# Spread accumulating DMAs, later LayerNorm steps, products at the start and a new last tile in a hybrid decoder step

## The chip, the cores and the metric

The kernel runs on one core of a Trainium2 chip. The metric is device time in microseconds (us) of one execution. A core has a tensor engine (PE, TensorE), a vector engine (DVE), a scalar engine (ACT), a general engine (POOL, GpSimd) and a queue engine (SP), each with its own program, and 16 DMA engines that all of them share. DMAs issued by SP or ACT appear in the profile as hardware queues, those issued by POOL as a software queue.

## What is computed

One layer of a hybrid decoder is run on 2048 prompt tokens and on 64 sample tokens (8 sequences of 8), all in float32, with width 1024:

```python
proj = x @ w_in                                  # 1024 -> 3584: q, f, i, g, B, C, h
o    = hgrn2(silu(q), f, i, state)               # gated linear recurrence, 4 heads of 128
o    = o * rsqrt(mean(o*o) + 1e-6) * onorm_g * silu(g)
yc   = B * conv3(C * h)                          # causal, 3 taps
x    = layer_norm(ALPHA * x + concat(o, yc) @ w_out)
hid  = square(relu(x @ w_ff1))                   # 1024 -> 4096
x    = layer_norm(ALPHA * x + hid @ w_ff2)       # 4096 -> 1024
```

It returns x for both groups, the recurrence's new states and the last rows of the convolution's input.

## The kernel before

**Blocks and stages.** The prompt is taken in four blocks `b` of 512 tokens; block 1 takes the 64 sample tokens along. The mixers of a block are the stages m1 (q and f of the four heads), m2 (i and g) and m3 (the convolution), written as generators of 16, 16 and 24 steps. The loop over `main()` (L862) calls one step after another and, between them, advances the recurrence (`rec_step`), issues DMAs and runs one waiting step of the block before (`pump`). The output projection m4 follows, then the first LayerNorm, FF1 and FF2.

**float32 products.** Each operand is split into a high part (by ACT, L164 or L203) and a low part (by DVE, L165 or L210), and one product becomes three (L239 to L241, L245 to L247). A weight tile of 512 KB is loaded into a staging buffer `st` by SP (three buffers), split into `wh` and `wl` (four buffers each) and used once. `weights(i)` splits up to three tiles ahead of the one it returns, and SP's next load waits until DVE's split has freed a buffer. ACT and DVE run their programs strictly in order.

**Sums of weights.** FF1 and FF2 use products of sums of quarters of their weights (seven products in place of eight). The sums T1 to T4 of each of eight chunks lie in DRAM scratch, `T_a` for FF1 and `T_b` for FF2. They are made in block 0 by POOL's DMAs: a copy (L349), or a copy that accumulates (L347). For one chunk this is eight DMAs in a fixed order, `make_sums` (L342):

```python
(("T1","B11",False), ("T3","B22",False), ("T1","B12",True), ("T3","B12",True),
 ("T2","T3",False),  ("T2","B11",True),  ("T4","T2",False), ("T4","B21",True))
```

Four chunks are made together, step by step. `making` holds 64 of these DMAs (T_b of chunks 0 to 3 and T_a of chunks 4 to 7, in pairs) and `making1` 48 (T_b of chunks 4 to 7, then T_a of chunks 2 and 3). POOL can have eight such DMAs on their way; the next waits for the one eight before. `hold(x)` (L354) makes POOL read one element of `x` first, so that the DMAs behind it in POOL's queue start only when that value exists.

**When they are issued.** From step 6 of block 0's mixers two per step, until the 64 are used up. Then, behind each of the eight plain units of FF1's first part, two of `making1`; in FF2's first part one every third step (held by the split value `h`, three buffers); in FF1's second part one for each of the first eight units; the rest in block 1's mixers. T_b of chunks 0 to 3 is needed first in FF2's first part of block 0, T_a of chunks 4 to 7 in FF1's second part, T_b of chunks 4 to 7 in FF2's second part, and T_a of chunks 2 and 3 in block 1.

**Other work on POOL.** The powers -0.5 of the norms run on POOL: L720 for the recurrence's output (`out_stages`, four tokens' tiles a block, needed by m4), L271 for LayerNorms. They stand in the same queue as the DMAs.

**The second LayerNorm of a block** is not done at its end but pushed to `bg` as three steps a tile, `a1` (statistics, L266 to L271), `a2` (L287) and `a3` (L290 and the store), which `pump` runs in the next block's mixers on every second step, from step 0 on. A tile's buffer `tok` (eight in all) is free after the store, and m2 needs four or five of them.

**The end.** In block 3 the last chunk of FF2 is worked tile by tile: for each of four tiles and each half of the columns twelve products, an add to x (L1242) and half of the statistics (L266). `scaled` (ACT, L1364) and `stored` (L1370 on DVE, L1371 on POOL, store by SP) of a tile are called inside the next tile's turn. The last tile has its own lines, L1390 to L1398.

Of the kernel before, what the change touches and what calls it, by code (L numbers as in the profile page):

```python
# [14 lines left out]
ALU = mybir.AluOpType  # L15
# [46 lines left out]
def hybrid_step(ctx, tc, a, o):  # L62
# [294 lines left out]
    making1 = chain(make_sums(quarter2, range(NPART, NCH)), make_sums(quarter1, range(NPLAIN, NPART)))  # L357
# [42 lines left out]
    load_constants()  # L400
    carry = None


    for b in range(NB):
# [456 lines left out]

        for i, _ in enumerate(main()):  # L862
            rec_step()
            if b == 0 and i >= 6:
                if i == 6:

                    hold(ks[0][:, 0:1])
                next(making, 0)
                next(making, 0)
            if b == 1 and i % 2 == 0:  # L870
                next(making1, 0)
            if i >= 16 and i % (3 if samp else 4) == 0:
                rec_step()
            if i % 2 == 0:
                pump()
# [314 lines left out]

        for f, w in twice(pl["f0"], 0):
            ff1(f, w, [(0, 256)])
        drain()
# [4 lines left out]
        for f, w in twice(pl["f0"], 1):  # L1198
            ff1(f, w, [(256, ncols - 256)])
        drain()  # L1200
# [65 lines left out]
        for part, (ff1_units, ff2_units) in enumerate(pl["parts"]):  # L1266
            queue += [(step, c) for step, c, _ in ff2_units]
            for i, (step, c, u) in enumerate(ff1_units):
                if part == 1 and i in (4, 12):
                    norm_weights(1, (i // 8,))  # L1270
                if len(ff1_units) - 5 <= i < len(ff1_units) - 3:
                    prepare()
                if b == 0 and part == 0:
                    if i == 0:
                        for _ in making:
                            pass
                    ff1(step, weights(u), segs)
                    hold(values(c)[:, 0, 0, 0:1])
                    next(making1, 0)
                    next(making1, 0)  # L1280
                else:
                    ff1_product(step, c, weights(u))
                    if b == 0 and i < 8:
                        hold(values(c)[:, 0, 0, 0:1])
                        next(making1, 0)
# [18 lines left out]
            for n_, (step, c, u) in enumerate(ff2_units):  # L1304
# [21 lines left out]
                if b == 0 and part == 0 and n_ % 3 == 0:  # L1326
                    hold(h[:, 0, 0:1].bitcast(F32))
                    next(making1, 0)
# [23 lines left out]
        if b == NB - 1:  # L1352
# [13 lines left out]
            def stored(t):  # L1366
                for dh in range(2):
                    ds_ = slice(dh * 512, dh * 512 + 512)
                    z = x1[t][:, ds_]
                    v.tensor_tensor(z, z, lnb[:, 0, ds_], ALU.mult)  # L1370
                    g.tensor_tensor(z, z, lnb[:, 1, ds_], ALU.add)  # L1371
                    nc.sync.dma_start(dst(t)[:, ds_], z)

            for t in range(nt):
# [13 lines left out]
                ln_rstd(sts[t], P)  # L1388
            t, st = nt - 1, sts[nt - 1]
            v.scalar_tensor_tensor(st[:, 16:17], st[:, 12:13], -1.0, st[:, 15:16], ALU.mult, ALU.mult)  # L1390
            lo, hi = x1[t][:, :512], x1[t][:, 512:]
            s.activation(lo, lo, AF.Identity, scale=st[:, 15:16], bias=st[:, 16:17])
            v.scalar_tensor_tensor(hi, hi, st[:, 12:13], lnb[:, 0, 512:], ALU.subtract, ALU.mult)
            v.scalar_tensor_tensor(hi, hi, st[:, 15:16], lnb[:, 1, 512:], ALU.mult, ALU.add)
            nc.sync.dma_start(dst(t)[:, 512:], hi)
            v.tensor_tensor(lo, lo, lnb[:, 0, :512], ALU.mult)
            v.tensor_tensor(lo, lo, lnb[:, 1, :512], ALU.add)
            nc.scalar.dma_start(dst(t)[:, :512], lo)  # L1398
# [88 lines left out]
```

## Time and profile before

| | |
|---|---|
| median of 3 runs | 2387.24 us (2386.88 to 2389.86) |
| profiled execution | 2390.55 us |
| its span, first to last instruction | 2388.3 us |
| mean granted clock of TensorE | 0.994 |
| TensorE busy | 2340.0 us (98%) |
| DVE busy | 1785.6 us (75%) |
| ACT busy | 1233.5 us (52%) |
| POOL busy | 184.9 us (8%) |
| moved by DMA | 418.89 MB |

The times in the profile are those of the profiled execution, which took 3.3 us more than the median. A row of grouped instructions gives line, engine, operation, tiles (out<-in), busy time and the engine's idle time before them with what ended it. A wait is written "who <- for whom: us in total, times, longest". In a table by stage each engine has its busy time and its number of instructions, followed by the granted clock (1.00 is full speed), the DMA engines' mean busy share and the rate. A TensorE that runs at half clock counts as busy.

### The profile page before, as it was taken

The numbers are of one execution on the slowest core, as the hardware profiler recorded it, in microseconds if no ns is written. First come the engines' busy times: TensorE is split into PE (matmuls) and PEld (weight loads), VectorE is DVE, ScalarE is ACT, GpSimd is POOL, SyncE is SP. The second block draws the span as 40 slices with busy tenths as digits, with TensorE's granted clock in tenths as the row PEclk, the third lists the DMA queues.
The fourth block names the chain that finished last, engine by engine and source line by source line (L and its number), as shares of the span: only waits on it lengthen the run. The fifth ranks groups of instructions, "written<-read, shape, count | busy, mean of one in ns | idle before, by whom it ended". The sixth has DMA issues, their size and how long they took to land.

```text
span 2388.3 us, 38146 instructions
## 1 busy us (share of the span) xinstructions
PE 2340.0 (98%) x15036; PEld 2043.1 (86%) x15036; DVE 1785.6 (75%) x2832; ACT 1233.5 (52%) x1922; POOL 184.9 (8%) x234
## 2 busy tenths in 40 slices
PE   8999999999999999999999999999999999999998
PEld 7778978988879889879878788998988788998996
DVE  7856858578785677875688956888588975888678
ACT  5324645565423446646654234665665324665563
POOL 2230021100101110000000000000000001000001
PEclk9999999999999999999999999999999999999999
DMA  8997598867633644545553325456665325456663
GB/s 285 264 282 214 151 266 273 257 200 211 163 107 78 172 149 133 168 150 177 177 177 109 99 71 194 155 187 197 192 210 163 102 79 172 141 176 203 200 191 119
DMA packets 131507, 418.89 MB, mean 175 GB/s; under 512 B 13376, under 2 KB 17856, under 8 KB 131328
## 3 DMA queue, kind: packets, MB, share of 16 engines
q1 hardware_dynamic: 108880, 347.96, 45.7%
q0 software_dynamic: 22016, 67.71, 11.5%
q8 instruction: 118, 1.93, 0.3%
q10 hardware_dynamic: 432, 0.79, 0.1%
q14 instruction: 61, 0.50, 0.1%
HBM read 405.36 MB, written 69.77 MB: 199 GB/s over the span
## 4 chain that ended last, share of the span: by engine, by line
PE 50%; DVE 5%; DMA 1%; issue 1%; ACT 1%; POOL 0%; POOLq 0%; DVEq 0%; ACTq 0%
PE ps L247 9%; PE ps L245 9%; PE ps L246 9%; PE ps L239 6%; PE ps L240 6%; PE ps L241 6%; DVE wl L210 1%; DMA st<-in_w_ff 1%; PE ps L683 1%; PE ps L250 1%; PE ps L251 1%; DVE S L603 0%; DMA st<-T_b 0%; DVE l L165 0%; ACT wh L203 0%
## 5 line engine op out<-in xcount | busy, mean ns | idle before, releaser
L210 DVE TENSOR_TENSOR wl<-st,wh 128x1024 fp32r<-128x1024 f32 x580 | 707.4, 1221 | 173.3 <-ACT wh L203 171.2
L203 ACT ACTIVATE wh<-st 128x1024 fp32r<-128x1024 f32 x581 | 612.9, 1055 | 352.1 <-PE ps L247 125.6
L239 PE MATMUL ps<-X,wh 128*128 128x256 f32 (+2 forms) x1376 | 466.6, 339 | 9.8 <-ACT X L164 8.3
L240 PE MATMUL ps<-X,wh 128*128 128x256 f32 (+2 forms) x1376 | 456.8, 332 | 0.3 <-DVE X L165 0.3
L241 PE MATMUL ps<-X,wl 128*128 128x256 f32 (+2 forms) x1376 | 456.3, 332 | 0.0
L247 PE MATMUL ps<-wh,l 128*128 128x512 f32 x868 | 340.8, 393 | 9.0 <-DVE l L165 8.6
L245 PE MATMUL ps<-wh,h 128*128 128x512 f32 x868 | 338.2, 390 | 0.0
L246 PE MATMUL ps<-wl,h 128*128 128x512 f32 x868 | 338.0, 389 | 0.0
L239 PEld LDWEIGHTS ps<-X,wh 128*128 128x128 f32 x1376 | 263.0, 191 | 35.0 <-ACT X L164 9.3
L241 PEld LDWEIGHTS ps<-X,wl 128*128 128x128 f32 x1376 | 262.8, 191 | 22.0
L240 PEld LDWEIGHTS ps<-X,wh 128*128 128x128 f32 x1376 | 263.2, 191 | 21.3 <-DVE X L165 1.5
L247 PEld LDWEIGHTS ps<-wh,l 128*128 128x128 f32 x868 | 162.9, 188 | 52.4 <-DVE l L165 19.0
L246 PEld LDWEIGHTS ps<-wl,h 128*128 128x128 f32 x868 | 163.0, 188 | 34.0
L245 PEld LDWEIGHTS ps<-wh,h 128*128 128x128 f32 x868 | 163.0, 188 | 33.1 <-ACT h L164 0.4
L165 DVE TENSOR_TENSOR l<-raw,h 128x512 fp32r<-128x512 f32 x217 | 148.2, 683 | 9.8 <-ACT h L164 9.8
L247 PE MATMUL ps<-X,wl 128*128 128x256 f32 (+1 forms) x528 | 152.1, 288 | 0.2 <-DVE wl L210 0.2
L246 PE MATMUL ps<-X,wh 128*128 128x256 f32 (+1 forms) x528 | 151.9, 288 | 0.0
L245 PE MATMUL ps<-X,wh 128*128 128x256 f32 (+1 forms) x528 | 151.9, 288 | 0.0
L271 POOL TENSOR_TENSOR sm<-sm,nhalf 128x1 f32<-128x1 f32 (+1 forms) x34 | 34.7, 1020 | 1475.8 <-DVE sm L270 1429.6
L1147 DVE TENSOR_TENSOR raw<-raw,ps 128x512 f32<-128x512 f32 (+1 forms) x112 | 61.0, 571 | 104.9 <-PE ps L247 104.7
L164 ACT ACTIVATE h<-raw 128x512 fp32r<-128x512 f32 x217 | 133.7, 616 | 2.3 <-PE ps L246 2.2
L239 PE MATMUL ps<-wh,X 128*128 128x512 f32 x256 | 105.8, 413 | 2.8 <-DVE S L603 2.8
(259 smaller groups left out, 4369.2 us busy)
## 6 DMA issues: line engine op xcount, KB each, us to landing
st<-in_w_ff SPq DMA_DIRECT2D x227, 512.0 KB, 3.7
st<-T_b SPq DMA_DIRECT2D x124, 512.0 KB, 3.7
st<-in_w_in SPq DMA_DIRECT2D x110, 512.0 KB, 3.9
st<-T_a SPq DMA_DIRECT2D x88, 512.0 KB, 3.5
st<-in_w_out SPq DMA_DIRECT2D x56, 512.0 KB, 4.5
T_b<-in_w_ff POOLq DMA_DIRECT2D x48, 512.0 KB, 14.7
T_a<-in_w_ff POOLq DMA_DIRECT2D x36, 512.0 KB, 19.1
T_b<-T_b POOLq DMA_DIRECT2D x16, 512.0 KB, 12.9
```

The lines of the kernel that those rows point to most:

```text
L164: s.activation(hi, src, AF.Copy)
L165: later.append(lambda: v.tensor_tensor(lo, src, hi.bitcast(F32), ALU.subtract))
L203: s.activation(wh, st, AF.Copy)
L210: v.tensor_tensor(wl, st, wh.bitcast(F32), ALU.subtract)
L239: te.matmul(out, lh, rh, start=first, stop=False)
L240: te.matmul(out, lh, rl, start=False, stop=False)
L241: te.matmul(out, ll, rh, start=False, stop=last)
L245: te.matmul(out, lh, rh, start=first, stop=False, skip_group_check=True)
L246: te.matmul(out, lh, rl, start=False, stop=False, skip_group_check=True)
L247: te.matmul(out, ll, rh, start=False, stop=last, skip_group_check=True)
L271: g.tensor_tensor(st[:n, 15:16], st[:n, 14:15], nhalf[:n, 0:1], ALU.pow)
L1147: v.tensor_tensor(z, z, ps, (ALU.add, ALU.subtract)[op - 2])
```

## The change

It has four parts.

1. **DMAs of the sums.** Block 0's mixers issue only 26 steps' worth (52 DMAs). The other 12 of the first 64, and then T_b of chunks 4 to 7, are issued in FF1 (both passes of the plain first units, then FF1's first part) by `sums_beside`, one or two for a unit, each time held by a read of the value that the unit before wrote. In FF2's first part one is issued every third step. FF1's second part issues none; T_a of chunks 2 and 3 comes wholly in block 1's mixers (16 DMAs where 13 were).
2. **LayerNorm steps.** `pump` is called on every third step for as many tiles as must free their buffer before m2 (two tiles in block 1, one in block 2, none in block 3) and on every second step from step 26 on.
3. **Start.** TensorE gets twelve products of `ones` into a bank that nobody reads, ahead of the first weight.
4. **End.** `stored` adds on DVE instead of POOL, and the last tile is done by four passes of DVE, two that need only the mean and two that need the power, instead of L1390 to L1397.

The diff, cut to what matters:

```diff
-    making1 = chain(make_sums(quarter2, range(NPART, NCH)), make_sums(quarter1, range(NPLAIN, NPART)))
+    all_sums = chain(making, make_sums(quarter2, range(NPART, NCH)))
+    making1 = make_sums(quarter1, range(NPLAIN, NPART))
...
+    idle = PS((P, 4, P))
+    for _ in range(12):
+        te.matmul(idle, ones, ones.unsqueeze(1).to_broadcast([P, 4, P]), start=True, stop=True)
...
+        first_steps = 3 * max(0, len(bg) // 3 + nt + (1 if samp else 0) - 8)
...
-            if b == 0 and i >= 6:
+            if b == 0 and 6 <= i < 32:
...
-                next(making, 0)
-                next(making, 0)
+                next(all_sums, 0)
+                next(all_sums, 0)
...
-            if i % 2 == 0:
+            if i % 3 == 2 and first_steps:
+                first_steps -= 1
+                pump()
+            elif i >= 26 and i % 2 == 0:
                 pump()
...
+        def sums_beside(f, half, n):
+            if b == 0:
+                if made:
+                    hold(made.pop())
+                    for _ in range(n):
+                        next(all_sums, 0)
+                made.append(values(f // FC)[:, 2 * (f % FC // 2) + half, f % 2, 0:1])
...
             ff1(f, w, [(0, 256)])
+            sums_beside(f, 0, 1 + f % 2)
...
             ff1(f, w, [(256, ncols - 256)])
+            sums_beside(f, 1, 1 + f % 2)
...
-                    if i == 0:
-                        for _ in making:
-                            pass
                     ff1(step, weights(u), segs)
-                    hold(values(c)[:, 0, 0, 0:1])
-                    next(making1, 0)
-                    next(making1, 0)
+                    sums_beside(step, 1, 1 + i % 2)
                 else:
                     ff1_product(step, c, weights(u))
-                    if b == 0 and i < 8:
-                        hold(values(c)[:, 0, 0, 0:1])
-                        next(making1, 0)
...
-                if b == 0 and part == 0 and n_ % 3 == 0:
+                if b == 0 and part == 0 and n_ % 3 == 2:
                     hold(h[:, 0, 0:1].bitcast(F32))
-                    next(making1, 0)
+                    if next(all_sums, 0) == 0:
+                        next(making1, 0)
...
-                    g.tensor_tensor(z, z, lnb[:, 1, ds_], ALU.add)
+                    v.tensor_tensor(z, z, lnb[:, 1, ds_], ALU.add)
...
-            v.scalar_tensor_tensor(st[:, 16:17], st[:, 12:13], -1.0, st[:, 15:16], ALU.mult, ALU.mult)
-            lo, hi = x1[t][:, :512], x1[t][:, 512:]
-            s.activation(lo, lo, AF.Identity, scale=st[:, 15:16], bias=st[:, 16:17])
-            v.scalar_tensor_tensor(hi, hi, st[:, 12:13], lnb[:, 0, 512:], ALU.subtract, ALU.mult)
-            v.scalar_tensor_tensor(hi, hi, st[:, 15:16], lnb[:, 1, 512:], ALU.mult, ALU.add)
-            nc.sync.dma_start(dst(t)[:, 512:], hi)
-            v.tensor_tensor(lo, lo, lnb[:, 0, :512], ALU.mult)
-            v.tensor_tensor(lo, lo, lnb[:, 1, :512], ALU.add)
-            nc.scalar.dma_start(dst(t)[:, :512], lo)
+            halves = [slice(dh * 512, dh * 512 + 512) for dh in range(2)]
+            for ds_ in halves:
+                z = x1[t][:, ds_]
+                v.scalar_tensor_tensor(z, z, st[:, 12:13], lnb[:, 0, ds_], ALU.subtract, ALU.mult)
+            for ds_, queue_ in zip(halves, (nc.sync, nc.scalar)):
+                z = x1[t][:, ds_]
+                v.scalar_tensor_tensor(z, z, st[:, 15:16], lnb[:, 1, ds_], ALU.mult, ALU.add)
+                queue_.dma_start(dst(t)[:, ds_], z)
```

SP's order of loads and TensorE's order of products stay as they were, but for the twelve products. Three places show how the rest moves. The line numbers after the change are higher by 6 from the mixers on (L720 becomes L726, L634 becomes L640).

First, POOL's queue in block 0 where the powers of the recurrence's output stand (`sm`, `nhalf`). Before, they come behind the last of the 64 DMAs:

```order
L347 DMA T_b_121<-in_w_ff 128x1024
L347 DMA T_a_105<-in_w_ff 256x1x512
L347 DMA T_b_125<-in_w_ff 128x1024
L347 DMA T_a_109<-in_w_ff 256x1x512
L347 DMA T_b_129<-in_w_ff 128x1024
L347 DMA T_a_113<-in_w_ff 256x1x512
L720 TENSOR_TENSOR sm_1673<-sm_1673,nhalf 128x4
```

Now they come behind the 52nd:

```order
L349 DMA T_b_117<-T_b_115 128x1024
L349 DMA T_a_101<-T_a_99 128x1024
L349 DMA T_b_121<-T_b_119 128x1024
L349 DMA T_a_105<-T_a_103 128x1024
L726 TENSOR_TENSOR sm_1674<-sm_1674,nhalf 128x4
```

The powers moved ahead of 12 DMAs, four copies and eight that accumulate.

Second, POOL's queue at the turn from FF1's first part to FF2's first part in block 0 (`tick<-raw` is a read of an FF1 value, `tick<-h` one of a split value of FF2). Before:

```order
L354 TENSOR_TENSOR tick<-raw_3118 128x1
L347 DMA T_b_140<-in_w_ff 128x1024
L347 DMA T_b_144<-in_w_ff 128x1024
L354 TENSOR_TENSOR tick<-h_3063 128x1
L349 DMA T_b_131<-T_b_132 128x1024
L354 TENSOR_TENSOR tick<-h_3296 128x1
L349 DMA T_b_135<-T_b_136 128x1024
```

Now:

```order
L354 TENSOR_TENSOR tick<-raw_3155 128x1
L347 DMA T_b_135<-in_w_ff 128x1024
L347 DMA T_b_139<-in_w_ff 128x1024
L354 TENSOR_TENSOR tick<-h_3305 128x1
L347 DMA T_b_143<-in_w_ff 128x1024
L354 TENSOR_TENSOR tick<-h_3375 128x1
L349 DMA T_b_133<-T_b_131 128x1024
```

At the same point of FF2 the sums of chunks 4 to 7 are eight DMAs further on: 35 DMAs stand between the first LayerNorm's powers and the first read of h, where 16 stood.

Third, DVE in block 2's m1, where the recurrence of two heads is under way (`S` are its tiles, `wl` a weight's low part). Before, with a step of a LayerNorm in it:

```order
L455 TENSOR_TENSOR S_12700<-ps_12640,S_12701 128x512
L634 TENSOR_TENSOR S_12738<-S_12569,S_12620 128x512
L651 TENSOR_TENSOR S_12569<-S_12569,S_12619 128x512
L287 SCALAR_TENSOR_TENSOR tok_8321<-tok_8321,sm_12682,lnb 128x1024
L693 COPY_PREDICATED S_12464<-masks,ps_12762 32x4x2x8 x4
L613 TENSOR_TENSOR S_12386<-S_12386,S_12465 128x32x8
```

Now:

```order
L461 TENSOR_TENSOR S_12704<-ps_12650,S_12705 128x512
L640 TENSOR_TENSOR S_12742<-S_12581,S_12630 128x512
L657 TENSOR_TENSOR S_12581<-S_12581,S_12629 128x512
L699 COPY_PREDICATED S_12480<-masks,ps_12765 32x4x2x8 x4
L619 TENSOR_TENSOR S_12399<-S_12399,S_12481 128x32x8
```

The third tile's step has left this place; in block 2 only the first tile's three steps stay in m1.

More of the change, by code (lines that the diff above doesn't have):

```diff
@@ L400, in hybrid_step @@
     load_constants()
+    idle = PS((P, 4, P))
+    for _ in range(12):
+        te.matmul(idle, ones, ones.unsqueeze(1).to_broadcast([P, 4, P]), start=True, stop=True)
+    idle = None
     carry = None
@@ L1188, in hybrid_step @@
         to = dict(PRODUCTS)
+        made = []
+        def sums_beside(f, half, n):
[5 more added lines that the diff above has]
+                made.append(values(f // FC)[:, 2 * (f % FC // 2) + half, f % 2, 0:1])
         for f, w in twice(pl["f0"], 0):
             ff1(f, w, [(0, 256)])
+            sums_beside(f, 0, 1 + f % 2)
         drain()
```

## The prediction

> **What bounds the kernel now.** I read the page first, then TensorE's waits, then busy time by stage, and last the stages in which TensorE waited. The page's head:
>
> ```profile
> span 2388.3 us, 38146 instructions
> ...
> PE 2340.0 (98%) x15036; PEld 2043.1 (86%) x15036; DVE 1785.6 (75%) x2832; ACT 1233.5 (52%) x1922; POOL 184.9 (8%) x234
> ...
> q1 hardware_dynamic: 108880, 347.96, 45.7%
> q0 software_dynamic: 22016, 67.71, 11.5%
> ```
>
> TensorE is busy for all but 48.3 us of the span. Its own work stays (the change adds only 12 products at the start), so the gain can only come from those 48.3 us, and from stretches at half clock, which count as busy. TensorE's waits over the whole run (line waited for: us in total, times, longest) say where they are:
>
> ```profile
> ...
> PE ps L239 <- ACT X L164: 8.3, 2, 6.7
> PE ps L729 <- DVE S L725: 6.1, 2, 3.1
> PE ps L245 <- ACT raw L1145: 4.5, 2, 3.5
> PE ps L239 <- DVE S L603: 3.8, 3, 1.4
> PE ps L683 <- ACT tok L506: 2.7, 2, 1.4
> ```
>
> Busy time by stage places them. The columns are TensorE, weight loads, DVE, ACT, POOL, the granted clock, the DMA engines' share and GB/s.
>
> ```profile
> 172.30:180.00 7.70, 1.67 (x9) 0.93 (x7) 3.96 (x7) 5.52 (x26) 5.02 (x4) 0.82 1.08 193
> 177.20:184.00 6.80, 3.91 (x12) 3.23 (x13) 3.57 (x6) 6.13 (x24) 2.66 (x2) 0.50 1.06 219
> 256.00:297.00 41.00, 41.00 (x341) 40.78 (x340) 35.75 (x39) 29.29 (x50) 0.81 (x1) 1.00 0.50 147
> 345.00:360.00 15.00, 12.42 (x53) 9.41 (x52) 8.32 (x11) 6.32 (x8) 2.49 (x5) 1.00 1.04 319
> 440.00:460.00 20.00, 15.30 (x123) 14.63 (x122) 9.15 (x9) 12.78 (x16) 2.90 (x5) 1.00 0.95 303
> 1296.00:1338.00 42.00, 39.39 (x334) 30.41 (x332) 40.50 (x92) 12.60 (x20) 2.88 (x4) 1.00 0.28 88
> 1337.80:1344.60 6.80, 6.47 (x51) 5.27 (x52) 6.35 (x19) 2.69 (x5) 0.16 (x1) 0.50 0.43 157
> 1400.00:1450.00 50.00, 50.00 (x277) 43.02 (x276) 27.01 (x53) 22.05 (x66) 5.74 (x4) 1.00 0.36 114
> ```
>
> Three kinds of loss stand there. In block 0 the DMA engines are full (share 1.04 to 1.08) where TensorE waits. At 1296 DVE is full (40.50 of 42 us) with nearly idle DMA engines. And behind two of the waits the clock is 0.50 for 6.8 us.
>
> **1. The wait at 172.9 (-8.1 us).** POOL's timeline (start, duration, line, idle before):
>
> ```profile
> 145.30 0.52 POOL L349 DMA_DIRECT2D T_a<-T_a  x1 [4.09 <-DMA T_a<-in_w_ff]
> ...
> 172.32 1.05 POOL L347 DMA_DIRECT2D T_a<-in_w_ff  x1 [0.44 <-DMA T_a<-T_a]
> 172.91 2.52 POOL L720 TENSOR_TENSOR sm<-sm,nhalf 128x4 f32<-128x4 f32 x2
> ...
> ACT S L723 <- POOL sm L720: 12.9, 2, 10.8
> ```
>
> The power of L720 stands in POOL's queue behind all 64 sum DMAs; the last is issued at 172.32 and L720 runs right after. ACT had waited up to 10.8 us for it, and TensorE then 6.1 us in two waits. The change puts 52 DMAs ahead of it. The 52nd of before is issued at 145.30, so POOL is free 27 us earlier and the wait goes. What is late next is nothing of POOL's: in block 2 the same stage, without DMAs on POOL, has TensorE at 50.00 of 50 (row 1400). The half clock behind it costs at most 3.4 us; part of those 6.8 us is the second wait itself, so I take 2.0. 6.1 + 2.0 = 8.1; the least is 6.1.
>
> **2. The wait at 455 (-4.5 us).** At the start of FF1's second half three first-half sums (T_a) are still copied, and a weight tile that is due takes far longer to land than alone (DMA issues by stage: bytes, us to landing; the first row is 250 to 300, without software DMAs, the second 345 to 360, the third 445 to 460):
>
> ```profile
> st<-in_w_ff SPq DMA_DIRECT2D x14, 512.0 KB, 3.6
> ...
> st<-in_w_ff SPq DMA_DIRECT2D x4, 512.0 KB, 7.9
> ...
> st<-in_w_ff SPq DMA_DIRECT2D x3, 512.0 KB, 8.4
> ```
>
> 3.6 us become 8.4. After the change no sum is issued from the last step of FF2's first half until block 1, so this 4.5 us goes; at worst, if the last sums spill over, 2 of it.
>
> **3. The other end of that: FF1 and FF2 of block 0 (+4.0 us).** This is the cost, and the least certain term. The 12 delayed and 23 further sum DMAs now lie in FF1 of block 0, each held by a read of a value. The price of one: 11.5% of 2388 us is 275 us of all engines; less the outputs on that queue, 112 sums cost about 2.2 us each. A weight tile costs 45.7% of 2388 us over 347.96 MB, or 1.64 us for 512 KB. From 256 to 345 there are 89 us of DMA time, 93 at the measured 1.05. The weights take 20.5 (share 0.50 of 41 us) and then 8 times 1.64, 34 in all, and leave 59 us, or 27 sums. 35 are asked for. So about 8 sums, 18 us of DMA time, are still open when FF2 starts; before, only 16 sums had been asked for by then. FF1 itself has slack: its units wait for weights that were split three units earlier. FF2 has little, because the split h of a step stands on ACT behind the split of a weight three steps ahead, and that behind its landing:
>
> ```profile
> L210 DVE TENSOR_TENSOR wl<-st,wh 128x1024 fp32r<-128x1024 f32 x580 | 707.4, 1221 | 173.3 <-ACT wh L203 171.2
> ```
>
> One step is 12 products of 0.227 us, 2.72 us. A staging buffer is free again after 7.9 us of landing, ACT's pass, DVE's of 1.22 us and the next issue, about 10.5 us; with three of them one weight comes per 3.5 us, and 0.8 us is lost a step. Before, this cost 2.6 us in 345 to 360 (12.42 busy of 15). After, 18 us beside weights that take 1.64 of every 3.5 us last some 32 us, 9 steps, and about 7 us are lost. The difference is +4. It would be -2.6 if the backlog is gone by 345, and +15 if it stays through half of FF2. The Trainium skill (DMA: Bandwidth & Descriptors, Queues, rings and completion order) says each DMA engine goes round its queues packet by packet; by that rule alone a weight tile would get half an engine, an estimate of 5.2 us to landing, and the term would be about -2.6. The rows show 7.9, so they decide.
>
> **4. The LayerNorm steps moved out of m1 (-7.5 us).** In block 2's m1 stage DVE runs these beside the recurrence (1290 to 1340, busy us and mean ns):
>
> ```profile
> L290 DVE SCALAR_TENSOR_TENSOR tok<-tok,sm,lnb 128x1024 f32<-128x1024 f32 x3 | 3.8, 1262 | 0.0
> ...
> L266 DVE BATCH_NORM_STATS2 sm<-tok 128x6 f32<-128x512 f32 x4 | 2.6, 683 | 0.0
> L287 DVE SCALAR_TENSOR_TENSOR tok<-tok,sm,lnb 128x1024 f32<-128x1024 f32 x2 | 2.6, 1277 | 0.0
> ...
> ACT S L636 <- DVE S L634: 26.5, 6, 10.0
> ```
>
> 9 us of DVE's work there are LayerNorm, and ACT waits up to 10.0 us for DVE's L634, then TensorE for banks. After the change only one of the five tiles is normalised early in block 2, none in block 3; the rest starts at step 26. That frees about 8 us of DVE ahead of waits of 1.4 us each. The waits for L603 and L506 total 3.8 + 2.7; 1.0 of it is block 1's, so 5.5 us are at stake, and the half clock at 1337.8, at most 3.4, taken as 2.4 because the small products of this stage do not follow the clock alone: 7.9, of which I take 7.5. What hides the moved work: DVE has 23 us free in 1400 to 1450, and four tiles of 4.3 us (two statistics, L287, L290, small ones), 17 us, spread over steps 26 to 48. If that cover fails, a step of 1.26 us ahead of a bank's release costs up to 1.3 us, a few times. In block 1 six steps (two tiles) move to the end of m2, where one wait of 1.0 us stands already: 0, from -2 to +3.
>
> **5. The start (-2.2 us).** The first products:
>
> ```profile
> 6.69 0.80 PE L239 MATMUL ps<-X,wh 128*128 128x512 f32 x1 [6.69 <-ACT X L164]
> ...
> 8.73 4.30 DVE L165 TENSOR_TENSOR X<-tok,X 128x512 fp32r<-128x512 f32 x7 [1.29 <-ACT X L164]
> ...
> 11.78 0.63 PE L239 MATMUL ps<-X,wh 128*128 128x512 f32 x1
> ...
> 12.20 0.63 PE L240 MATMUL ps<-X,wh 128*128 128x512 f32 x1
> ...
> 13.91 0.39 PE L239 MATMUL ps<-X,wh 128*128 128x512 f32 x1
> ...
> 14.14 0.40 PE L240 MATMUL ps<-X,wh 128*128 128x512 f32 x1
> ```
>
> From 6.69 to 13.4 products stand 0.42 us apart, later 0.23. Twelve idle products at 0.42 take 5.1 us and fit into the 6.69 us of loading. Warm, the first 24 are bound by DVE, whose last split ends at 13.03: they end near 13.5 instead of 15.8. So -2.2; 0 if the clock falls back while the first tiles trickle in. The Trainium skill (TensorE: Matmul & The Clock Gate, Part 1) gives about 3.4 us of sustained activity until the full clock; by that, an estimate of 1.6 us is saved. The trace took 6.7 us, with gaps in the first half.
>
> **6. The tail (+1.7 us).** The end of the loop on DVE:
>
> ```profile
> 2373.79 0.68 DVE L1242 TENSOR_TENSOR tok<-tok,ps 128x512 f32<-128x512 f32 x1
> ...
> 2376.81 0.16 DVE L1363 SCALAR_TENSOR_TENSOR sm<-sm 128x1 f32<-128x1 f32 x1 [1.18 <-POOL sm L271]
> ...
> 2378.29 1.29 DVE L1370 TENSOR_TENSOR tok<-tok,lnb 128x512 f32<-128x512 f32 x2
> 2379.50 0.68 DVE L1242 TENSOR_TENSOR tok<-tok,ps 128x512 f32<-128x512 f32 x1
> ...
> 2384.72 0.69 DVE L1397 TENSOR_TENSOR tok<-tok,lnb 128x512 f32<-128x512 f32 x1
> ```
>
> A tile's turn is 5.71 us, a chain through POOL, ACT and DVE. Two more adds on DVE (1.3 us) stand in it; POOL answers some 0.5 us sooner without its own adds. Three turns add 1.3 + 0.9 + 0.9 = 3.1. The last tile took 5.9 us from its last sum at 2379.50 to the end of L1397. It now takes the two statistics, the small steps and four passes of 0.7, 4.6 us, of which the first two run while POOL makes the power: -1.4. Net +1.7, from -0.5 to +2.5.
>
> **The sum.** -8.1 - 4.5 + 4.0 - 7.5 + 0 - 2.2 + 1.7 = -16.6 us. The profiled execution took 2390.55 us (span 2388.3, 2.25 around it), 3.3 above the median 2387.24; 2390.55 - 16.6 = 2373.95, and from the median 2370.6.
>
> **Rivals.**
> A: *Only the queue is freed* (0.12). The m1 waits are the recurrence's own and stay, and the clock at the start falls back: -8.1 - 4.5 + 4.0 + 1.7 = -6.9, 2380. For it: the recurrence fills DVE at 1296 with 31 us besides LayerNorm. Against: the waits come only after three tiles' steps.
> B: *Slower* (0.05). POOL falls behind its DMAs in FF1, so its reads of h come late; h has three buffers, and ACT's next split waits for POOL, and the engines stay full through all of FF2. 28 steps at 0.8 us and a first wait of 10 to 15 us: 22 + 13, less the 2.6 of before, +32 in place of +4, 2399. It decides from about 12 sums open at FF2's start: eight may be on the way without holding POOL, and the balance of part 3 says eight. For it: that balance is close. Against: weights tolerate delay in FF1.
> C: *Nothing gained* (0.05). L720 waits for DVE's L719, not for its place in the queue, or DVE's moved steps cost in m2 what m1 gains: 2386. Against: L720 follows the last DMA within 0.6 us.
> The forecast has 0.78; within it term 3 alone moves the time by -6.6 to +11 us.
>
> **Range and chances.** About 0.2% (4.8 us) is what a measurement of this kernel can tell from no change. Low end: terms 3 and 4 at their best, 2370.6 - 6.6 - 2.4 - 2.2 is 2359. High end: term 3 at +15 (2381) or rival A (2380). Faster by over 0.2%, under 2382.5: the forecast but for 0.02 and A, 0.88; same 0.07 (C and the rest); slower 0.05 (B).
>
> **What would show it.** No TensorE wait for the out stage near 172 and no clock of 0.50 there; no wait for the first products of FF1's second half; more DMA share than 0.50 in 256 to 297, and the wait for l in 345 to 380 of about 7 us; DVE below full in block 2's m1 and no 0.50 there; products 0.23 us apart from 7 us on; a tile's turn of 6.6 us in the tail. I am wrong if the split of h waits for POOL's reads, or if TensorE waits appear in m2.

## The result and the profile after

The changed kernel took 2372.82 us (median of 4 runs, 2372.06 to 2376.58) against 2387.44 us before (4 runs, 2386.88 to 2389.86): 14.6 us less, ratio 0.993 with an interval of 0.9914 to 0.9946. The forecast was 2370.6 us. On a second occasion, with nine runs of the kernel before beside it, the changed kernel took 2372.81 us again, and the kernel before 2394.12 (2388.70 to 2398.96): ratio 0.9915 (0.9898 to 0.9932), 21.3 us less. The eight runs of the changed kernel on the two occasions lie within 4.9 us, the thirteen of the kernel before within 12.1, which turned out to be a part of the answer.

The profiled execution of the changed kernel took 2372.06 us (span 2370.3). The head of its page:

```profile
span 2370.3 us, 38176 instructions
...
PE 2335.7 (99%) x15048; PEld 2039.4 (86%) x15048; DVE 1789.1 (75%) x2837; ACT 1232.6 (52%) x1921; POOL 186.1 (8%) x234
```

TensorE's idle time fell from 48.3 to 34.6 us although it does 12 products more, and its busy time fell by 4.3 us all the same, because less of it runs at half clock (the mean granted clock rose from 0.994 to 0.997). Its waits over the whole run (line waited for: us in total, times, longest):

```profile
PE ps L247 <- DVE l L165: 10.3, 15, 1.5
PE ps L250 <- DVE hp L165: 3.2, 3, 1.3
PE ps L239 <- ACT X L164: 2.3, 2, 1.6
PE ps L689 <- DVE S L626: 1.9, 2, 1.0
...
PE ps L239 <- DVE S L609: 1.0, 1, 1.0
PE ps L705 <- DVE S L620: 1.0, 2, 0.5
```

The 6.1 us for the out stage, the 4.5 us for raw and the 2.7 us for tok are no longer there. The wait for l grew from 8.6 to 10.3. New are two lines that wait for the recurrence's S on DVE (L626 and L620), 2.9 us. (New line numbers from the mixers on are 6 higher than those of before.) The same stages as in the prediction, in the changed kernel:

```profile
164.00:175.00 11.00, 11.00 (x64) 9.40 (x63) 6.36 (x12) 7.35 (x28) 2.92 (x2) 1.00 0.16 49
245.00:286.00 41.00, 41.00 (x340) 40.74 (x339) 34.16 (x37) 27.80 (x47) 18.83 (x33) 1.00 1.03 286
334.00:372.00 38.00, 34.70 (x147) 26.72 (x146) 28.69 (x37) 19.48 (x25) 8.50 (x14) 1.00 0.94 301
432.00:447.00 15.00, 15.00 (x127) 15.00 (x127) 8.55 (x9) 10.94 (x15) 0.00 (x0) 1.00 0.69 241
1281.50:1323.50 42.00, 42.00 (x382) 33.01 (x381) 36.70 (x90) 15.38 (x23) 0.00 (x0) 1.00 0.28 89
1323.00:1330.00 7.00, 7.00 (x61) 5.53 (x60) 5.51 (x15) 1.06 (x1) 0.00 (x0) 1.00 0.00 1
1340.00:1372.00 32.00, 30.57 (x298) 23.17 (x296) 30.23 (x72) 9.34 (x13) 1.72 (x3) 1.00 0.31 99
```

TensorE (the first column behind the length) is full through the out stage, FF1, the start of FF1's second half and block 2's m1. FF1 of block 0 now carries the sums, with the DMA engines at 1.03 instead of 0.50. Two rows are not full: the start of FF2 (334 to 372) and, not foreseen in the sum, block 2's m2 (1340 to 1372), where DVE is busy for 30.23 of 32 us.

### A ledger by the same product

TensorE does the same products in the same order in all these kernels, but for the idle ones at the start. So the nth product from the end is the same work in every trace, and the difference of its start between two traces says what has been gained up to there. Below, each trace is set against that of the kernel before; a column is a stretch, by the times of the kernel before, and a number is what the stretch cost more (+) or less (-). "after" and "again" are two executions of the changed kernel; the first four rows do not have the spread sums, the others do.

```
stretch (us)   6-  160- 336- 430- 500- 690- 890- 920-  1320- 1372- 1590- 1740- 1880- 1930- 1960-  tail
               20  200  430  475  560  725  920  1320  1350  1400  1620  1800  1930  1960  2360
before          0    0    0    0    0    0    0    0     0     0     0     0     0     0     0     0
norm alone   -1.8 +1.8 +2.5 +4.2 +1.1    0    0    0   -6.0  +1.7  -0.9  +0.5  -3.1  +1.6  +0.4     0
start alone  -3.0 -0.8 +3.0 +2.4 +0.1 -1.5    0  +0.6  -2.8     0  -0.9  +1.0  +2.8     0     0     0
tail alone   -0.8 -0.9 +1.9 +2.1 -0.6 -1.5 -1.5  +0.3     0     0  -0.9  +1.6  +1.6     0     0  +2.0
sums alone   -1.0 -8.3 +4.3 -5.3 +0.7 -1.5    0  +0.2  -2.8     0  -0.9  +0.9  +1.5     0  +0.1     0
after        -3.0 -8.3 +3.4 -5.6 +0.3 -1.5    0  +0.1  -6.0  +1.7  -0.9  +0.5  -3.1  +1.6  +0.4  +2.4
again        -3.1 -8.3 +3.0 -5.6 +0.8 -1.5    0  +0.5  -6.0  +1.6  -0.9     0  -3.1  +1.6  +0.3  +2.5
```

The row "after" adds up to the difference of the spans, -18.0, but for rounding. Every step of the prediction has its column: start, out stage, FF2, FF1's second half, block 1 (690), block 2 (m1 from 1320, m2 from 1372), block 3 (m1 from 1880, m2 from 1930), tail. A row can also differ in a stretch that its edit does not touch, as -2.8 and +2.8 for "start alone" in blocks 2 and 3: that is how far one execution differs from another.

### The profile page after: what moved, and what is told of

Same layout as the page of the kernel before. It is cut to its first block, busy times and chain, and to the rows that moved or that the text cites. A ratio compares the mean times of both kernels' runs of the same rounds, so it can differ in the third digit from the quotient of the medians.

```text
span 2370.3 us, 38176 instructions
## 1 busy us (share of the span) xinstructions
PE 2335.7 (99%) x15048; PEld 2039.4 (86%) x15048; DVE 1789.1 (75%) x2837; ACT 1232.6 (52%) x1921; POOL 186.1 (8%) x234
## 4 chain that ended last, share of the span: by engine, by line
PE 53%; DVE 3%; issue 1%; DMA 1%; ACT 0%; POOL 0%; DVEq 0%; ACTq 0%; POOLq 0%
PE ps L247 10%; PE ps L245 9%; PE ps L246 9%; PE ps L239 7%; PE ps L240 7%; PE ps L241 7%; PE ps L689 1%; DVE wl L210 1%; PE ps L250 1%; PE ps L251 1%; DVE tok L1267 0%; DMA st<-T_b 0%; DVE l L165 0%; PE ps L783 0%; PE ps L780 0%
## 5 line engine op out<-in xcount | busy, mean ns | idle before, releaser
L247 PE MATMUL ps<-wh,l 128*128 128x512 f32 x868 | 341.5, 393 | 11.0 <-DVE l L165 10.3
```

Of the source, the lines that this page charges most:

```text
L247: te.matmul(out, ll, rh, start=False, stop=last, skip_group_check=True)
```

## The experiments

In each expectation P is the theory held first, Q and R are its rivals.

**The four parts, each alone on the kernel before.** They ran beside 29 runs of the kernel before (median 2393.91 us, 2385.59 to 2400.75). The four differences of the medians add up to 18.7 us (15.6 + 2.7 + 2.2 - 1.8), between the 14.6 and the 21.3 us of the whole change.

The spread of the sums alone (the mixers stop after 52 DMAs, the rest is held by reads in FF1 and FF2, as in the change's diff):

```
-            if b == 0 and i >= 6:
+            if b == 0 and 6 <= i < 32:
...
-                next(making, 0)
+                next(all_sums, 0)
...
+            sums_beside(f, 0, 1 + f % 2)
```

> The kernel before with the spread of the accumulating DMAs alone (old start, old LayerNorm steps, old tail). Theory P (the parts are independent, each brings what the two traces show in its stage when the same product is compared): the waits at 172.9 and 176.8 us and the half clock behind them go, -8.3; the FF2 stage of block 0 (340 to 420 us) loses 3.4 more than before; the waits at 448 and 455 us go, -5.5; nothing else moves. Sum -10.4 us, 2377 us. In block 2 the two waits near 1334 us and the 6.8 us of half clock behind them are still there. Rival Q (only the freed POOL queue counts, the other two terms depend on the moved start and cancel): -8.3 or less, 2379 to 2382 us. Rival R (delayed sums pile up in FF1): FF2's loss is 10 us or more, 2384 us.

Measured: 2378.32 us (2377.22 to 2378.88), ratio 0.9936 (0.9924 to 0.9948). By the trace it was as theory P said: -8.3, +4.3, -5.3, and both of block 2's waits still there (block 3's too), as the waits show:

```profile
PE ps L239 <- DVE S L604: 3.8, 3, 1.4
...
PE ps L684 <- ACT tok L507: 2.7, 2, 1.4
```

The half clock behind them did not come in this execution, though (-2.8). By the medians it gained 15.6 us, not 10.4, and its five runs lie within 1.7 us while the 29 of the kernel before lie over 15. Most of that kernel's unsteadiness sits in FF2 and FF1's second half of block 0: its four executions without the spread sums differ there by up to 6.6 us (336 to 475), while FF1's second half is within 0.3 us in every execution that spread the sums and put none of them there.

The times of the LayerNorm steps alone:

```
-            if i % 2 == 0:
+            if i % 3 == 2 and first_steps:
+                first_steps -= 1
+                pump()
+            elif i >= 26 and i % 2 == 0:
                 pump()
```

> The kernel before with the new times of the LayerNorm steps alone. Theory P: in m1 of block 2 -6.0 us and in its m2 +1.65 (new waits of 0.7 and 1.1 us on DVE's S where one step of 1.28 us stands ahead), in block 3 -3.1 and +1.6, together -5.8 us; block 1 is 0 as far as the steps go, and -1.5 if its wait near 706 us happens to lie across two clock windows. 2380 to 2381.6 us. Rival Q (the m1 waits are the recurrence's own and the traces differ by luck of the clock): at most -2 us, 2385 us.

Measured: 2391.18 us (2384.44 to 2394.43), ratio 0.9986 (0.9975 to 0.9997), so between 0.7 and 6 us. The time alone could hardly tell P from Q; the ledger does, with -6.0, +1.7, -3.1, +1.6 as P said and no -1.5 in block 1. The waits for ACT's tok (2.7 us) are gone, and of the 3.8 us for DVE's L603 only block 1's are left:

```profile
PE ps L239 <- DVE S L603: 1.0, 1, 1.0
```

Theory Q falls, though it is right in part: how much of the half clock follows these waits is luck. Block 2's m1 cost 2.8 us less than in the trace of before in two executions whose steps were not moved ("start alone", "sums alone"), and block 3's m1 1.5 to 2.8 us more in three of them. The wait of block 2 in the kernel before, and the same wait in "sums alone", where it lies across two windows and the clock stays:

```profile
1334.34:1337.75 3.41, 1.05 (x4) 0.49 (x3) 3.38 (x7) 0.57 (x2) 0.57 (x1) 1.00 0.53 154
```

```profile
1323.06:1326.47 3.41, 1.84 (x7) 0.86 (x6) 3.38 (x5) 0.00 (x0) 0.00 (x0) 1.00 0.28 103
1326.47:1329.88 3.41, 2.23 (x45) 1.93 (x46) 3.41 (x8) 3.19 (x6) 0.57 (x1) 1.00 0.52 209
```

Against the mean of the four executions whose steps were not moved, the moved steps bring 4.6 us in m1 of each of the two blocks, not 6.0 and 3.1. The waits of this kernel in the stretch that it does not touch were larger than in the trace of the kernel before (first that trace from 345 to 475 us, then this one):

```profile
PE ps L245 <- ACT raw L1145: 4.5, 2, 3.5
PE ps L247 <- DVE l L165: 2.6, 2, 1.4
```

```profile
PE ps L247 <- DVE l L165: 4.6, 4, 1.6
PE ps L245 <- ACT raw L1151: 3.7, 2, 2.9
PE ps L245 <- ACT wh L203: 1.7, 1, 1.7
```

The twelve idle products at the start alone:

```
+    idle = PS((P, 4, P))
+    for _ in range(12):
+        te.matmul(idle, ones, ones.unsqueeze(1).to_broadcast([P, 4, P]), start=True, stop=True)
+    idle = None
```

> The kernel before with the 12 idle products at the start alone. Theory P: the clock is full from about 5.4 us instead of 13.4, the 24th product starts near 12.2 us instead of 15.3: -3.0 us, 2384.4 us, and the distance stays the same to the end. Rival Q: a later wait takes it back (the wait at 172.9 us is for POOL's queue behind 64 DMAs, whose pace is not that of TensorE): the -3.0 at 20 us is gone at 185 us, 2387 us.

Measured: 2391.71 us (2385.68 to 2398.20), ratio 0.9993 (0.9982 to 1.0004), which decides nothing by itself. In the ledger the -3.0 are there at 20 us and still there behind the wait at 172 us (-3.8): P, not Q. But three other kernels without those products also stood 0.8 to 1.8 us ahead of the trace of before at 20 us: the clock rose at 10.3 to 12.6 us in them and at 13.4 in that one.

The new tail alone (the diff is the tail's part of the change):

```
-                    g.tensor_tensor(z, z, lnb[:, 1, ds_], ALU.add)
+                    v.tensor_tensor(z, z, lnb[:, 1, ds_], ALU.add)
```

> The kernel before with the new tail alone. Theory P: a tile's turn in the tail goes from 5.71 to 6.69 us, three turns and the first tile +3.4 us at the last tile's last sum, then -0.9 from there to the end: +2.5 us, 2389.9 us. Rival Q: the two adds that moved to DVE are hidden there and only the shorter last tile counts: -0.9 us, 2386.5 us.

Measured: 2395.69 us (2392.05 to 2398.79), ratio 1.0007 (0.9996 to 1.0018), which by itself tells nothing; from the start of the last product to the end it takes 11.66 us instead of 9.63, so +2.0. That is nearer to P's +2.5 than to Q's -0.9: this part makes the tail slower.

**Variants of the changed kernel.** They ran beside the unaltered one:

> The changed kernel unaltered, as the yardstick of the three variants that run beside it. Theory P (the waits of FF2 and FF1 in block 0 vary from execution to execution in the kernel before, and the spread of the sums ends that): its times lie within about 2 us of each other, near 2373 us, while those of the kernel before lie over some 10 us, and its gain is 17 to 20 us against this chip's before, not 14.6. Rival Q (the spread is the chip's and meets every kernel): the changed kernel's times lie over 10 us too.

Measured: 2372.81 us (three runs within 0.9 us, one at 2376.96) against 2394.12, so 21.3 us faster than the kernel before. P but for the one run: 4.7 us are more than its 2, and less than the 10.3 of the nine runs beside them.

The add of the tail back on POOL, the new last tile kept:

```
                     v.tensor_tensor(z, z, lnb[:, 0, ds_], ALU.mult)
-                    v.tensor_tensor(z, z, lnb[:, 1, ds_], ALU.add)
+                    g.tensor_tensor(z, z, lnb[:, 1, ds_], ALU.add)
```

> The changed kernel with the last add of a tail tile back on POOL, and the new last tile kept. Theory P (the adds moved to DVE stand in the chain of each tile's turn): the turn of a tile goes back to 5.7 us, the last sum follows the last product by 0.8 us instead of 4.2, and the last tile still takes 7.9 us from there: -3.4 us against the changed kernel. Rival Q (the turn is set by the reads of the tile's banks or the power on POOL): the adds on POOL delay POOL's power by 0.5 us a tile, and less than 1.5 us comes back.

Measured: 2367.77 us (2366.92 to 2368.29), ratio 0.9889 (0.9874 to 0.9905) to the kernel before. From the start of the last product to the end it takes 8.76 us, where the changed kernel takes 12.08: -3.3, as P said; the other 1.7 us lie in FF2. DVE's timeline of the changed kernel and of this variant (start, duration, line):

```profile
2355.71 0.68 DVE L1267 TENSOR_TENSOR tok<-tok,ps 128x512 f32<-128x512 f32 x1
...
2359.73 0.69 DVE L1388 TENSOR_TENSOR tok<-tok,lnb 128x512 f32<-128x512 f32 x1
...
2361.79 0.69 DVE L1389 TENSOR_TENSOR tok<-tok,lnb 128x512 f32<-128x512 f32 x1
2362.40 0.68 DVE L1267 TENSOR_TENSOR tok<-tok,ps 128x512 f32<-128x512 f32 x1
```

```profile
2351.49 0.68 DVE L1267 TENSOR_TENSOR tok<-tok,ps 128x512 f32<-128x512 f32 x1
...
2357.22 0.68 DVE L1267 TENSOR_TENSOR tok<-tok,ps 128x512 f32<-128x512 f32 x1
```

From the last sum of one tile to that of the next it is 6.69 us with the adds on DVE and 5.73 without. With the adds on DVE the last product starts 4.2 us before the last sum (0.8 us without): the sum stands behind four passes of the tile before (two of L1388, two of L1389).

The LayerNorm steps held until step 38, then one a step:

```
-            elif i >= 26 and i % 2 == 0:
+            elif i >= 38:
```

> The changed kernel with the LayerNorm steps that wait for step 26 held until step 38 (about 1371 us in block 2), then one a step instead of one in two. Theory P (the new waits near 1363 and 1367 us and near 1919 and 1923 us come of single LayerNorm steps that stand ahead of the recurrence while DVE is 95% busy): both pairs go, -1.65 and -1.58, -3.2 us against the changed kernel. Rival Q (the recurrence itself is late there by then, since m1 now runs at TensorE's pace): the waits stay or come back some 10 us later, 0 to -1 us; crowding after step 38 may even cost 1 to 3 us.

Measured: 2371.49 us (2369.44 to 2373.39). The pairs of waits in m2 are gone, and one new wait of the same size stands in each of the two blocks (block 2, 1340 to 1420 us; block 3 has the same row):

```profile
PE ps L735 <- DVE S L731: 1.5, 1, 1.5
```

So neither theory alone: the waits do come of the steps' place, and crowding them gave it all back.

The reads of h kept in FF2, their DMAs moved into FF1's second half:

```
                     hold(h[:, 0, 0:1].bitcast(F32))
-                    if next(all_sums, 0) == 0:
-                        next(making1, 0)
...
                     ff1_product(step, c, weights(u))
+                    if b == 0 and i >= 2:
+                        hold(values(c)[:, 0, 0, 0:1])
+                        next(all_sums, 0)
```

> The changed kernel with the reads of h by POOL kept in FF2 of block 0, but the sum DMAs that they release moved on into FF1's second half (ten of them, one a unit from the third on, each behind a read of a value). Theory P (FF2 loses time because its weight tiles land late beside sum DMAs): the backlog from FF1 still costs the waits up to 358 us, about 3.5 us, but the rest of FF2's loss (0.9 us at 405 and the 1.5 us around 362 to 372) goes; FF1's second half, which splits its weights three units ahead, takes the ten DMAs at no cost: -1.5 to -2.4 us. Rival Q (POOL's reads of h hold its buffers): FF2's loss of 5.6 us stays, 0. Rival R (sum DMAs in FF1's second half cost what they did in the kernel before, where three copies at its start made 3.7 us): +2 to +5 us.

Measured: 2381.09 us (2380.68 to 2383.38), 8.3 us slower than the changed kernel. FF2's column falls to -0.4 from +3.0 in the unaltered one, with POOL's reads still in place: the loss there is the DMAs, not the reads, as P said. In FF1's second half R was right, and worse: from -5.6 to +2.3 in 430 to 475 us, and +2.7 more in 500 to 560. Two of its weight tiles landed 15.1 us after their issue (median, 436 to 460 us) instead of 3.5 in the changed kernel (420 to 447 us), each kernel's row below, and TensorE waited for them:

```profile
st<-in_w_ff SPq DMA_DIRECT2D x2, 512.0 KB, 15.1
...
PE ps L245 <- ACT wh L203: 4.1, 1, 4.1
```

```profile
st<-in_w_ff SPq DMA_DIRECT2D x5, 512.0 KB, 3.5
```

Both tricks together, with the LayerNorm steps left out at 32 to 37 only:

```
-            elif i >= 26 and i % 2 == 0:
+            elif (26 <= i < 32 or i >= 38) and i % 2 == 0:
```

> The changed kernel with the last add of a tail tile on POOL as in the run with that alone, and with the LayerNorm steps of the mixers left out at steps 32 to 37 (they run at 26, 28, 30 and from 38 on, one in two as before). Theory P (one LayerNorm step, L287 of the second tile, stands ahead of the recurrence where DVE has no room, and in the run with all steps after 38 it was their crowding that made the new wait at L735): the pairs of waits near 1363 and 1919 us go and no wait of L735 appears: -3.2 us against the run with the add on POOL alone (2367.8), 2364.6 us. Rival Q (two of DVE's 8 to 12 us of moved steps must end up ahead of some bank's release wherever they stand): waits of the same 1.6 us a block show up elsewhere, 2367.5 us.

Measured: 2376.13 us (2372.15 to 2379.24), 8 us slower than the add on POOL alone. The pairs in m2 went, but behind the mixers 4.6 us were lost in block 2 and 6.9 in block 3, part of it at half clock. Neither theory had this. SP's queue shows it (1405 to 1432 us: start, duration, line; below it DVE's last LayerNorm step, and SP's wait for it):

```profile
1406.14 8.49 SPq L182 DMA_DIRECT2D st<-in_w_out  x2
1421.21 7.39 SPq L263 DMA_DIRECT2D lnb<-in_lnb  x2
...
1429.64 2.02 SPq L182 DMA_DIRECT2D st<-in_w_out  x3
```

```profile
1426.97 1.27 DVE L290 SCALAR_TENSOR_TENSOR tok<-tok,sm,lnb 64x1024 f32<-64x1024 f32 x1
```

```profile
SPq L263 <- DVE tok L290: 6.7, 1, 6.7
```

The second of the two reloads of lnb goes out as the last step that reads the old lnb (L290) ends, at 1428.2 us, and behind it in SP's queue stand weight tiles, three of them in this view, which TensorE then waits for. The LayerNorm steps have a deadline, and the change's own last step (L290 at 1413.45) meets it: its reloads are both out by 1418.4 us.

Steps at 26, 28, 30, 32, 38, 40, 42 to 46 and 48, so that none stands at 34 and 36 and the last is no later:

```
-            elif i >= 26 and i % 2 == 0:
+            elif i in (26, 28, 30, 32, 38, 40, 42, 43, 44, 45, 46, 48):
```

> The changed kernel with the last add of a tail tile on POOL, and LayerNorm steps at 26, 28, 30, 32, then at 38, 40, 42, 43, 44, 45, 46 and 48: none stands at 34 and 36, where the recurrence waited for DVE, and the last one is no later than in the changed kernel, so that the reload of lnb on SP's queue, which waits for the last reader, is no later either. Theory P (the moved steps cost where they stand ahead of the recurrence, and at the end where the reload of lnb and the weights behind it wait for them): the pairs near 1363 and 1919 us go, and neither the wait at L735 near 1407 nor the one near 1437 us appears: -3.2 us against the add on POOL alone (2367.8), 2364.6 us. Rival Q (DVE has no room for these steps anywhere between steps 32 and 48): a wait of 1 to 1.7 us a block comes back at another place, 2367 us or more.

Measured: 2366.91 us (2364.92 to 2371.11), ratio 0.9904 (0.9889 to 0.9918) to a kernel before of 2389.52 on that occasion. The m2 waits fell from 1.6 to 0.4 us in each of blocks 2 and 3, and no wait came back elsewhere in the mixers, -2.4 us by the trace: P, less a remainder. The time alone would have fitted Q (2367 or more); its FF2 happened to be 2.3 us slower than in the run with the add on POOL alone. This and that run are the best versions found; they can't be told apart.

64 sum DMAs in the mixers of block 0 again, in the changed kernel:

```
-            if b == 0 and 6 <= i < 32:
+            if b == 0 and 6 <= i < 38:
```

> The changed kernel with 64 sum DMAs in the mixers of block 0, as before, instead of 52 (the last 12 stand again ahead of the power of L726 in POOL's queue), and so 12 fewer in FF1 and FF2. Theory P (the wait at 172.9 us was the place in POOL's queue): the two waits and the half clock behind them return, +8.3 by 185 us; FF2's loss in 344 to 420 us, 3.4 to 5.6 us in the changed kernel, falls to 1 to 3 us, since fewer sums are open when it starts; sum +5 to +7, 2378 to 2380 us. Rival Q (the power waits for its input from DVE and the queue did not matter): nothing returns at 172.9 us, 2370 to 2373 us. Rival R (the loss of FF2 does not depend on how many sums FF1 has to carry): +8.3, 2381 us.

Measured: 2378.74 us (2373.27 to 2380.93), ratio 0.9942 (0.9927 to 0.9956): P. POOL's timeline of this variant, then that of the changed kernel:

```profile
166.62 0.81 POOL L347 DMA_DIRECT2D T_b<-in_w_ff  x1 [0.28 <-DMA T_b<-T_b]
167.82 1.05 POOL L347 DMA_DIRECT2D T_a<-in_w_ff  x1 [0.39 <-DMA T_a<-T_a]
168.41 2.54 POOL L726 TENSOR_TENSOR sm<-sm,nhalf 128x4 f32<-128x4 f32 x2
```

```profile
142.22 0.52 POOL L349 DMA_DIRECT2D T_a<-T_a  x1 [4.10 <-DMA T_a<-in_w_ff]
155.58 1.88 POOL L726 TENSOR_TENSOR sm<-sm,nhalf 128x4 f32<-128x4 f32 x1 [12.85 <-DVE sm L725]
```

In the first the power runs two at a time behind the last DMA, in the second POOL had been idle for 12.85 us when DVE's input came. The two waits (4.5 us) and the half clock came back, 7.0 us, and FF2's column fell to -0.9: with 12 sums fewer to carry, FF2 lost 3.9 us less than in the unaltered one, and its -0.9 lies below the 1.2 to 4.3 us of the eight executions that spread all of them.

Six idle products instead of twelve:

```
-    for _ in range(12):
+    for _ in range(6):
```

> The changed kernel with 6 idle products at the start instead of 12: they end near 3.6 us, and TensorE then rests until the first real product at 6.7. Theory P (the clock counts busy time in windows of 3.41 us, and a window with a rest in it does not raise it): the full clock comes only at 9 to 13 us, the 24th product starts at 14 to 15.3 us instead of 12.2, +2 to +3 us. Rival Q (some 2.5 us of products in the first window are enough to raise it and it stays up): 12.2 us, 0.

Measured: 2373.97 us in one run; at 20 us it stands 2.1 us behind the changed kernel. PE's timeline of it:

```profile
1.07 2.93 PE L405 MATMUL ps<-ones 128*128 128x512 f32 x6 [1.07 <-POOL ones L137]
...
11.75 0.63 PE L240 MATMUL ps<-X,wh 128*128 128x512 f32 x1
...
12.58 0.39 PE L239 MATMUL ps<-X,wh 128*128 128x512 f32 x1
```

The clock rose at 12.5 us, as late as with no idle products at all (10.3 to 13.4): P, by one run.

## Why the prediction was right, step by step

**1, the queue of POOL** (-8.1): -8.3, in every kernel with the spread sums, and undone by putting 12 DMAs back. Right in mechanism and size. Rival A (only this) falls with the LayerNorm run, rival C with the POOL timeline. C's 2386 us needed both of its conditions; with one of them its own terms give 2378 to 2379.

**2, the wait at 455** (-4.5): -5.6 against that trace. Its typical size is larger: in four executions without the spread sums the stretch cost 0, 4.2, 2.4 and 2.1 us against the trace, 2.2 on average, so the typical gain is 5.6 + 2.2, about 7.8 us. That it is the sum DMAs that delay the weights was shown by the run that put ten of them there.

**3, FF1 and FF2 of block 0** (+4.0): +3.4 against the trace. FF1 had the slack that was claimed (41.00 of 41). But the sizing failed in two ways. First, the eight open sums were not eight: at 334 us, where FF2 starts in the changed kernel, four were under way and two more of the 35 had yet to be issued, and in the kernel before, at 345, four were under way as well. So FF2 starts with six unfinished sums against four. POOL had waited for its own chain, one sum reading what another makes (second row: 30.0 us, one wait of 15.7 of them from 306 to 322 us; POOL's waits, 235 to 420 us):

```profile
POOL tick L354 <- ACT h L164: 48.7, 7, 10.3
POOL T_b L349 <- DMA T_b<-in_w_ff: 30.0, 7, 15.7
```

Ten more were issued in FF2 from 344 us on, eight of them behind reads of h, which waited for ACT (first row). Second, the trace of before was a lucky execution: without the spread sums FF2 cost 1.8 us more on average (0, 2.5, 3.0, 1.9), with them 2.7 (eight executions, 1.2 to 4.3). The typical price of the step is thus about 1 us, not 4; that this trace shows 3.4 is luck. The sign named for it, a wait for l of about 7 us, came out at 4.0 (335 to 420). Rival B, with ACT waiting for POOL's reads, did not happen: POOL waited for ACT. The Trainium skill's packet-by-packet rule (DMA: Bandwidth & Descriptors, Queues, rings and completion order) gave an estimate of 5.2 us to landing and -2.6 us; the tiles took 9.1 us at 334 to 349 us in the changed kernel:

```profile
st<-in_w_ff SPq DMA_DIRECT2D x4, 512.0 KB, 9.1
```

so the measurement decides against that estimate here; why the tiles take longer was not tried.

**4, the LayerNorm steps** (-7.5): in m1 -6.0 in block 2 and -3.1 in block 3 (4.6 each against the mean of the executions with the old steps), more than the 7.5 together, as DVE is no longer full there (36.70 of 42). The step that failed is the cover: "DVE has 23 us free in 1400 to 1450, and four tiles ... spread over steps 26 to 48". Steps 26 to 36 do not run there but, in the changed kernel, at 1332 to 1369 us, where DVE is nearly full (30.23 of 32 from 1340 on), and a step (L287) stands ahead of the recurrence:

```profile
1360.22 1.28 DVE L287 SCALAR_TENSOR_TENSOR tok<-tok,sm,lnb 128x1024 f32<-128x1024 f32 x1
...
1362.75 0.41 DVE L619 TENSOR_TENSOR S<-S,S 128x256 f32<-128x256 f32 x1
1363.08 0.41 DVE L620 TENSOR_TENSOR S<-S,S 128x256 f32<-128x256 f32 x1
```

That cost 1.65 and 1.6 us, near the price named for a failed cover (up to 1.3 us, a few times), but it was not in the sum, and the text called waits in m2 the sign of being wrong. Net -5.8. Block 1's -1.5 is no effect of the steps: three executions without moved steps have it too, and "norm alone" has it not. It is the clock (below).

**5, the start** (-2.2): -3.0 against the trace, whose clock rose late; against the mean of the four executions without warm-up, 2.1. The value was right for the typical execution. The Trainium skill (TensorE: Matmul & The Clock Gate, Part 1), by which about 3.4 us of sustained activity bring the full clock, gave 1.6; with the twelve products the clock rose at 5.3 to 7.1 us in nine executions, 4.2 to 6 us behind the first product at 1.07.

**6, the tail** (+1.7): +2.4. A turn takes 6.69 us as forecast (6.6), and the last sum comes 3.4 us later with respect to the last product. The last tile saves 0.96 us, not 1.4 (the prediction's own 5.9 less 4.6 give 1.3): that term was mis-sized.

The sum of -16.6 met -18.5 between the two profiled executions and -14.6 to -21.3 between medians, of which the lower is from four runs of the kernel before that stood at the fast end of its range. That the total came out so near is partly luck. Between the two traces, terms 1 to 3, the m1 part of term 4 and the start brought 4.3 us more than was set down, and the clock in block 1 another 1.5; the forgotten m2 waits and the tail cost 4.0 us more, which cancels most of it.

## What to carry to other kernels

Take the cover of moved work from the very stretch in which it will run, step by step, and look for its deadline too: here the last reader of a buffer held up a reload, and with it every weight tile behind that in the queue. DMA traffic is not free wherever weights are split well ahead of their use: FF1's first part took its sums at no loss (41.00 of 41 us), while ten of them cost FF1's second half, which splits as far ahead, 7.9 us. Its DMA engines had less room (a share of 0.69 without sums, against 0.50), which may be why; it was not tried. And issues that wait should not stand in a queue ahead of small steps that others need. Before a term is sized from one trace, ask whether its stretch is bound by contention: here such a stretch differed by up to 6.6 us from one execution to the next, and the same product compared across traces shows it where the run's total does not.

## What the runs showed of the hardware

A drop of the clock needs no idle window. The granted clock changes on a grid of 3.41 us whose phase differs from execution to execution. In the 14 profiled executions here (the two of the records and twelve experiments), every window at full clock in which TensorE was busy for 0.46 of the time or less, 25 of them, was followed by at least one window at half clock; none with 0.59 or more was; of 18 windows between 0.48 and 0.57, seven were. The same wait in block 1, near 700 us, is an example: inside one window in the kernel before (busy 1.95 of 3.41, then 0.50), across two in the changed kernel:

```profile
706.29:709.70 3.41, 1.95 (x31) 1.62 (x17) 3.19 (x10) 0.08 (x1) 0.00 (x0) 1.00 0.00 0
709.70:713.11 3.41, 3.41 (x16) 3.41 (x15) 3.38 (x6) 0.00 (x0) 0.00 (x0) 0.50 0.23 56
```

```profile
691.48:694.89 3.41, 2.39 (x44) 1.71 (x42) 3.15 (x7) 1.64 (x3) 0.59 (x1) 1.00 0.18 74
694.89:698.30 3.41, 2.97 (x23) 2.79 (x22) 3.32 (x10) 0.00 (x0) 0.00 (x0) 1.00 0.19 79
```

A single window at half clock cost about 1.5 us (block 1's column), so that by an estimate from these rows a wait of 1.7 us may cost 1.7 or 3.2 us by chance. The Trainium skill (TensorE: Matmul & The Clock Gate, Part 1) has the free-running window of 3413 ns, which agrees, and a drop after an idle window, which does not: windows that were 0.44 busy dropped it. What exactly counts as busy was not tried. Nor was it settled why the kernel before varies so much in FF2 of block 0: that its DMA engines are full there is shown (share 1.04 from 345 to 360 us), what decides an execution's luck is not. The occasions used different chips, and what the chip adds was not separated; 29 runs on one chip spread over 15 us.
